# Where tiles stand in on-chip memory: 256-byte lines, and transposed activations 64 or 192 bytes behind a line

## The chip, the cores and the metric

The kernel runs on one core of one Trainium2 chip. The core has five engines with instruction queues of their own: TensorE (PE: matrix multiplies; its weight loads are shown apart as PEld), VectorE (DVE), ScalarE (ACT), GpSimd (POOL) and SyncE (SP), which here only issues DMAs. Operands lie in on-chip memory (SBUF, 128 partitions), matmul results in PSUM. The metric is the device time of one execution in microseconds (us).

## The reference

One layer of a bidirectional encoder on a sequence of 1024 tokens with 1024 features, in float32:

```python
a = rmsnorm(h, norm_mix[l])
proj = a @ w_in[l]
y_att = windowed_gqa(aq, ak, av, attn_sink[l]) @ w_branch_attn[l]
y_gla = gla_branch(gq, gk, gv, gr, z_f, z_b, ...) @ w_branch_gla[l]
merged = jax.nn.sigmoid(g_att) * y_att + jax.nn.sigmoid(g_gla) * y_gla
h = h + merged @ w_out[l]
h = h + expert_choice_ffn(rmsnorm(h, norm_ffn[l]), w_router[l], w_exp_gate[l], w_exp_up[l], w_exp_down[l])
ple_gate = jax.nn.sigmoid(rmsnorm(h, norm_ple[l]) @ w_ple_gate[l])
h = h + ple_gate * (p[l] @ w_ple[l])
return rmsnorm(h, norm_final)
```

`windowed_gqa` is attention with 8 query and 2 key heads in a window of 128 tokens, `gla_branch` a chunked linear attention with 4 heads in both directions, and `expert_choice_ffn` lets each of 16 experts take 128 tokens and run a SwiGLU of width 1024 on them. The experts' weights alone are 16 x 12 MB.

## The kernel before

**Split products.** Every large product is computed with three matmuls on the type float32r (`mm3`, lines 108 to 111): an operand x is kept as a pair, hi (x rounded by a ScalarE cast) and lo = x - hi (a VectorE subtraction), and hi·hi, hi·lo and lo·hi are summed in PSUM. `split` (lines 105 and 106) makes the pair, so line 106 stands for nearly all casts and subtractions of the profile. Tiles of such a pair end in `_h` and `_l` (`xt_h`, `xt_l`), weights are `wh`, `wl` or `slot`.

**A matmul and its two operands.** Each matmul instruction comes with a weight load: the stationary operand (128 columns, here 512 bytes of each partition) is loaded into the array, and the moving operand (512 or 256 columns) streams through it. In a profile's row the names behind the arrow are "moving,stationary" in most rows (`slot,xt_h`: the weight piece moves, xt_h is stationary); the two are put in another order in a few (`aT_h,wh`: aT_h moves). While one matmul streams, the weight load of the next one runs.

**Stages.** (1) Norm and transposition of the input into `aT_h`, `aT_l`; key, value and query projections with 256 moving columns of weights and aT stationary (`proj_tok`); gate projections with 512 columns of aT moving and weights stationary (`proj_T`). (2) Windowed attention, and the product of its transposed output `atT` with its branch weights (`m1_half`). (3) Four heads of linear attention, with more `proj_tok` and `proj_T`. (4) The second branch product and the product with w_out, both of whose operands are `slot` tiles; router; choice of tokens. (5) 16 experts: for each, 128 tokens are gathered into `xg`, transposed on TensorE and split into the pair `xt`; gate and up products (xt stationary, weight pieces moving, 512 columns) give `hid`, which is transposed and split into `hT`; the down product (hT stationary) is scaled and added into DRAM by an indirect DMA. Weight pieces of 1 MB come through a ring of 17 raw buffers (`next_pool`, line 1160), loaded by SP as a buffer comes free, and are split by ACT, DVE and some by POOL. (6) The last gate with pair `nT` as stationary operand, and the final norm.

**Order of the work.** Each engine runs its queue in the order in which the code is written; tiles come from pools, which are stacked in memory from the left and from the right side, and a tile that takes another's place waits for the last reader of that one.

**Where tiles stand.** The class `Lines` (lines 36 to 51) wraps a pool and rounds each tile up to a multiple of 128 bytes per partition, so that every tile begins on a multiple of 128 bytes; the tiles `edge` and `edge_small` shift the pools on both sides to such a line. The pool `small` is left as it is. In the program as built, 1209 tiles begin 128 bytes above a multiple of 256 and 645 on a multiple of 256. The 128x8x128 pairs and the weight pieces are all in the first class, with these exceptions: `atT`, the query weights in the pool `wqp`, and `v_h`, `sh`, `sl`, `qT` of the attentions.

Of the kernel before, what the change touches and what calls it, by code (L numbers as in the profile page):

```python
# [9 lines left out]
F32 = mybir.dt.float32  # L10
F32R = mybir.dt.float32r
BF16 = mybir.dt.bfloat16
I32 = mybir.dt.int32
# [7 lines left out]
T = 1024  # L21
NT = 8
D = 1024
KC = 8
EPS = 1e-6
NE = 16
INV_FREQ = [float(500000.0 ** (-i / 8.0)) for i in range(8)]
C_QA, C_KA, C_QG, C_KG, C_VG, C_RG, C_Z, C_GA, C_GG = 0, 512, 768, 1280, 1792, 2816, 3840, 3872, 4896

EDGE_SMALL = 24
SIZE = {F32: 4, F32R: 4, I32: 4, BF16: 2, U8: 1}


class Lines:
# [2 lines left out]
    def __init__(self, pool):  # L39
        self.pool = pool  # L40

    def tile(self, shape, dt, **kw):
        n = math.prod(shape[1:])
        per = 128 // SIZE[dt]
        if n % per == 0:
            return self.pool.tile(shape, dt, **kw)
        t = self.pool.tile([shape[0], -(-n // per) * per], dt, **kw)[:, 0:n]
        if len(shape) == 2:
            return t
        names = "abc"[:len(shape) - 1]  # L50
        return t.rearrange(f"p ({' '.join(names)}) -> p {' '.join(names)}", **dict(zip(names, shape[1:])))


@contextmanager
def lines(pool):
    with pool as p:
        yield Lines(p)
# [3 lines left out]
def tile_hybrid_block(  # L61
# [14 lines left out]
    def pool(name, bufs=1, side=None, space=None):  # L76
        kw = {}
        if side:
            kw["side"] = side
        if space is not None:  # L80
            kw["space"] = space
        if space != DRAM:
            kw["reuse_waits"] = "tile"
        made = tc.tile_pool(name=name, bufs=bufs, **kw)
        return made if space is not None or name == "small" else lines(made)


    ctx.enter_context(tc.tile_pool(name="edge", bufs=1, side="right")).tile([128, 24], F32, name="edge")
# [1 line left out]
    small = ctx.enter_context(pool("small", bufs=3))  # L90
# [7 lines left out]
    def bank(tag="mm"):  # L98
        return ps.tile([128, 512], F32, tag=tag, name="ps_" + tag, bufs=BUFS[tag])
# [48 lines left out]

    sA = ExitStack()
    aT_pool = sA.enter_context(pool("aT", side="right"))  # L150
    aT_h = aT_pool.tile([128, KC, T], F32R, name="aT_h")
    aT_l = aT_pool.tile([128, KC, T], F32R, name="aT_l")


    sinkb = const.tile([128, 8], F32, name="sinkb")
# [300 lines left out]
    with pool("lp") as lp:  # L456
        one = lp.tile([128, 128], F32, name="one")
        nc.gpsimd.memset(one, 1.0)
        for h in range(4):
# [14 lines left out]
            for u in (3, 2, 1, 0):  # L474
                nc.vector.tensor_sub(lt[:, u], lm[:, u], lt[:, u])
                for c in range(4):
                    ls = slice(c * 128, c * 128 + 128)
                    a, b = lm[:, u, ls], lt[:, u, ls]
                    if c >= 2:
                        a, b = a[:, ::-1], b[:, ::-1]  # L480
# [12 lines left out]
    ap2 = sB.enter_context(pool("at2", bufs=2))  # L493
# [13 lines left out]
    atT = {}  # L507

    def attn_block(b):
        lo_b, hi_b = max(0, b - 1), min(NT - 1, b + 1)  # L510
        nk = hi_b - lo_b + 1
        if b % 4 == 0:
            atT[b // 4] = (ap2.tile([128, 4, 512], F32R, name="atT_h", bufs=1),
                           ap2.tile([128, 4, 512], F32R, name="atT_l", bufs=1))
        ah, al = atT[b // 4]
        qhl = qT[b]
        ks = slice(lo_b * 128, (hi_b + 1) * 128)
        n = nk * 128
        sinks = [v.rearrange("p (g c) -> p g c", g=2) for v in (sinkb, nsink)]
        for cp in range(2):  # L520
# [31 lines left out]
            for g in range(2):  # L552
                for c in range(2):
                    nc.vector.tensor_scalar(sm[g][c][:, 0:n], sm[g][c][:, 0:n], rd[:, g, c:c + 1],
                                            None, op0=ALU.mult)
# [523 lines left out]
            merge(srt)  # L1079
    sO.close()  # L1080
    eg = ctx.enter_context(pool("eg", bufs=2))


    gtl = o1.tile([NE, 2, 128], F32, name="gtl")
# [18 lines left out]
    for t in range(NT - 1):  # L1103
        n = NT - 1 - t
# [12 lines left out]
    st = {}  # L1117

    def tokens(e):
        oh = eg.tile([128, NT, 128], BF16, name="oh", bufs=1)  # L1120
        nc.vector.tensor_tensor(oh, posT[:, :, e:e + 1].to_broadcast([128, NT, 128]),
                                iot.unsqueeze(1).to_broadcast([128, NT, 128]), op=ALU.is_equal)
        pi = bank("a")
        for t in range(NT):
            nc.tensor.matmul(pi[:, 0:2], oh[:, t], tok[:, t], start=t == 0, stop=t == NT - 1)
        idx = eg.tile([128, 1], I32, name="idx", bufs=NE)
        ins = nc.vector.tensor_scalar(idx, pi[:, 0:1], pi[:, 1:2], None, op0=ALU.add).ins
        st[e] = dict(idx=idx)
        return ins
# [7 lines left out]
    for e in range(2):  # L1137
        found = tokens(e)
        if e == 0:
            gathered = gather(0)  # L1140
    gather(1)
    tokens(2)


# [10 lines left out]
    e2 = sE.enter_context(pool("e2", side="right"))  # L1155
# [8 lines left out]
    def transposed(src, th, tl, g):  # L1164

        pt = bank("tr")
        for c in range(4):
            nc.tensor.transpose(pt[:, c * 128:(c + 1) * 128],  # L1168
                                src[:, (g * 4 + c) * 128:(g * 4 + c + 1) * 128], ident)
        split(th[:, g * 4:g * 4 + 4], tl[:, g * 4:g * 4 + 4], pt.rearrange("p (c t) -> p c t", c=4))  # L1170
# [18 lines left out]
    def hl_pair(po, name, **kw):  # L1189
        return [po.tile([128, KC, 128], F32R, name=name + x, **kw) for x in ("_h", "_l")]  # L1190

    def begin(e, after=None):
        st[e]["xt"] = hl_pair(e2, "xt")
        col = st[e]["col"] = eg.tile([128, NE + 1], F32, name="col", bufs=NE)
        with tc.issue_after(after) if after else ExitStack():
            nc.scalar.copy(col, st[e]["xg"][:, D:TW])
        for g in range(2):
            transposed(st[e]["xg"], *st[e]["xt"], g)

    begin(0)  # L1200
    for e in range(NE):
        s = st[e]
        hid = e2.tile([128, D], F32, tag="hid", name="hid", bufs=2)
        hT = hl_pair(e2, "hT")
        for c in range(2):
            cc = slice(c * 512, c * 512 + 512)
            pg = bank("mm")
            for k2 in range(2):
                part(pg, s["xt"], w_eg[e], k2, c)
            silu = nc.scalar.activation(hid[:, cc], pg, AF.Silu, scale=s["col"][:, NE:NE + 1])  # L1210
            pu = bank("mm")
            for k2 in range(2):
                part(pu, s["xt"], w_eu[e], k2, c)
            nc.vector.scalar_tensor_tensor(hid[:, cc], pu, s["col"][:, NE:NE + 1], hid[:, cc], op0=ALU.mult, op1=ALU.mult)
            transposed(hid, *hT, c)
        pd = [bank("b"), bank("b")]
        for c in range(2):
            part(pd[c], hT, w_ed[e], 0, c)
            if c == 0 and e + 1 < NE:
                begin(e + 1, silu.ins)  # L1220
        if e + 2 < NE:
            gather(e + 2)
        if e + 3 < NE:
            tokens(e + 3)
        y = e2.tile([128, D], F32, tag="hid", name="y", bufs=2)
        for c in range(2):
            part(pd[c], hT, w_ed[e], 1, c)
            nc.scalar.mul(y[:, c * 512:c * 512 + 512], pd[c], s["col"][:, e:e + 1])
        nc.gpsimd.indirect_dma_start(out=h_d[:, :], in_=y, in_offset=None, compute_op=ALU.add,
                                     out_offset=bass.IndirectOffsetOnAxis(ap=s["idx"][:, 0:1], axis=0))  # L1230
# [18 lines left out]
    f2 = ctx.enter_context(pool("f2", bufs=2, side="right"))  # L1249
# [23 lines left out]

    def front(t):
        ht = hs_[t]
        nT = hl_pair(f2, "nT")
        for g in range(2):
            transposed(ht, *nT, g)
        junk = f2.tile([128, D], BF16, name="junk", bufs=1)
        ss = small.tile([128, 1], F32, name="ssf")  # L1280
        nc.scalar.activation(junk, ht, AF.Square, accum_out=ss)
        rs = rstd_of(ss, D)
        rh = small.tile([128, 1], F32, name="rsh", bufs=4)
        nc.vector.tensor_scalar(rh, rs, 0.5, None, op0=ALU.mult)
        F[t] = ht, nT, rh
# [65 lines left out]
```

## Time and profile before

| | |
|---|---|
| median of 3 runs | 1777.96 us (1777.29 to 1778.06) |
| the profiled execution: its own time | 1777.2 us |
| its span from first to last instruction | 1775.5 us |
| mean granted TensorE clock | 0.984 of 2.4 GHz |
| PE busy | 1670.3 us, 94% of the span |
| DVE, ACT, POOL busy | 1223.0, 930.0, 259.6 us |

A matmul's busy time in the profile is longer than the distance to the next one, because matmuls overlap in the pipeline and their ends are modelled. What one matmul costs is therefore read from starts: the time from the start of one to the start of the next in an unbroken run, which is called the pitch here. The timeline shows starts to 0.01 us, so a run of n matmuls gives its mean pitch to 0.01/n us.

### The profile page before, as it was taken

The numbers are of one execution on the slowest core, as the hardware profiler recorded it, in microseconds if no ns is written. First come the engines' busy times: TensorE is split into PE (matmuls) and PEld (weight loads), VectorE is DVE, ScalarE is ACT, GpSimd is POOL, SyncE is SP. The second block draws the span as 40 slices with busy tenths as digits, with TensorE's granted clock in tenths as the row PEclk, the third lists the DMA queues.
The fourth block names the chain that finished last, engine by engine and source line by source line (L and its number), as shares of the span: only waits on it lengthen the run. The fifth ranks groups of instructions, "written<-read, shape, count | busy, mean of one in ns | idle before, by whom it ended". The sixth has DMA issues, their size and how long they took to land.

```text
span 1775.5 us, 23683 instructions
## 1 busy us (share of the span) xinstructions
PE 1670.3 (94%) x8795; PEld 1355.7 (76%) x8795; DVE 1223.0 (69%) x2412; ACT 930.0 (52%) x1451; POOL 259.6 (15%) x233
## 2 busy tenths in 40 slices
PE   7998999999999999999988849999999999999997
PEld 6977766768898989888866637777777777777786
DVE  7546855542646464663458888888989889888776
ACT  4245555341525252541222227787877878777742
POOL 1013300000000000000034232112221121221110
PEclk9999999999999999999999969999999999999999
DMA  6032411415212121065442569999999999994611
GB/s 226 1 102 107 131 32 40 144 49 187 70 50 72 49 71 49 1 208 172 157 177 108 204 230 380 375 373 366 373 357 370 377 368 369 347 372 151 224 62 48
DMA packets 171740, 335.10 MB, mean 189 GB/s; under 512 B 9180, under 2 KB 41988, under 8 KB 171624
## 3 DMA queue, kind: packets, MB, share of 16 engines
q1 hardware_dynamic: 154912, 277.96, 44.5%
q0 software_dynamic: 14704, 53.17, 9.2%
q10 hardware_dynamic: 2008, 2.46, 0.4%
q8 instruction: 69, 1.13, 0.3%
q14 instruction: 47, 0.39, 0.1%
HBM read 290.50 MB, written 43.06 MB: 188 GB/s over the span
## 4 chain that ended last, share of the span: by engine, by line
PE 75%; DVE 13%; issue 5%; ACT 4%; DMA 2%; POOL 1%; DVEq 0%; SPq 0%; ACTq 0%; POOLq 0%
PE ps_mm L111 17%; PE ps_mm L110 17%; PE ps_mm L109 16%; PE ps_b L110 5%; PE ps_b L111 5%; PE ps_b L109 5%; DVE slot L106 3%; ACT slot L106 2%; PE ps_tr L1168 2%; DVE lm L481 1%; DVE cand L918 1%; DVE rs_y L133 1%; PE ps_a L533 1%; PE ps_tr L562 1%; PE ps_b L567 1%
## 5 line engine op out<-in xcount | busy, mean ns | idle before, releaser
L106 DVE TENSOR_TENSOR slot<-slot 128x1024 fp32r<-128x1024 f32 x349 | 451.6, 1327 | 66.8 <-ACT slot L106 63.4
L106 ACT CAST slot<-slot 128x1024 fp32r<-128x1024 f32 x392 | 401.2, 1051 | 92.9 <-PE ps_mm L111 68.2
L110 PE MATMUL ps_mm<-slot,xt_h 128*128 128x512 f32 x512 | 203.7, 398 | 4.1 <-DVE slot L106 1.9
L111 PE MATMUL ps_mm<-aT_h,wl 128*128 128x512 f32 x512 | 203.2, 397 | 0.0
L109 PE MATMUL ps_mm<-aT_h,wh 128*128 128x512 f32 x512 | 202.1, 395 | 1.2 <-ACT sgr L246 1.2
L110 PE MATMUL ps_mm<-aT_l,wh 128*128 128x512 f32 x512 | 202.9, 396 | 0.0
L111 PE MATMUL ps_mm<-slot,xt_l 128*128 128x512 f32 x512 | 201.5, 394 | 0.0
L109 PE MATMUL ps_mm<-slot,xt_h 128*128 128x512 f32 x512 | 200.2, 391 | 0.0
L106 POOL TENSOR_TENSOR slot<-slot 128x1024 fp32r<-128x1024 f32 x43 | 104.2, 2425 | 417.5 <-ACT slot L106 230.1
L110 PEld LDWEIGHTS ps_mm<-slot,xt_h 128*128 128x128 f32 x512 | 96.5, 188 | 35.3 <-DVE slot L106 8.1
L109 PEld LDWEIGHTS ps_mm<-slot,xt_h 128*128 128x128 f32 x512 | 96.6, 189 | 20.2
L109 PEld LDWEIGHTS ps_mm<-aT_h,wh 128*128 128x128 f32 x512 | 96.7, 189 | 18.6 <-ACT sgr L246 1.4
L111 PEld LDWEIGHTS ps_mm<-slot,xt_l 128*128 128x128 f32 x512 | 96.5, 188 | 18.5
L111 PEld LDWEIGHTS ps_mm<-aT_h,wl 128*128 128x128 f32 x512 | 96.8, 189 | 18.1 <-issue 1.2
L110 PEld LDWEIGHTS ps_mm<-aT_l,wh 128*128 128x128 f32 x512 | 96.6, 189 | 18.2 <-issue 1.2
L106 DVE TENSOR_TENSOR wl<-raw,wh 128x2048 fp32r<-128x2048 f32 (+1 forms) x29 | 61.5, 2121 | 63.8 <-ACT wh L106 63.8
L110 PE MATMUL ps_b<-slot,hT_h 128*128 128x512 f32 x256 | 102.2, 399 | 0.8 <-POOL slot L106 0.7
L109 PE MATMUL ps_b<-slot,hT_h 128*128 128x512 f32 x256 | 102.5, 401 | 0.0
L111 PE MATMUL ps_b<-slot,hT_l 128*128 128x512 f32 x256 | 101.7, 397 | 0.0
L106 ACT CAST wh<-raw 128x2048 fp32r<-128x2048 f32 (+1 forms) x30 | 52.0, 1734 | 91.1 <-PE ps_mm L110 86.9
L109 PE MATMUL ps_mm<-wh,aT_h 128*128 128x256 f32 x320 | 92.4, 289 | 1.6 <-DVE sgr L588 1.6
L111 PE MATMUL ps_mm<-wh,aT_l 128*128 128x256 f32 x320 | 91.2, 285 | 1.4 <-DVE aT_l L106 1.4
(378 smaller groups left out, 3613.6 us busy)
## 6 DMA issues: line engine op xcount, KB each, us to landing
slot<-in_w_exp_down_dram SPq DMA_DIRECT2D x64, 1024.0 KB, 8.4
slot<-in_w_exp_gate_dram SPq DMA_DIRECT2D x62, 1024.0 KB, 8.0
slot<-in_w_exp_up_dram SPq DMA_DIRECT2D x62, 1024.0 KB
raw<-in_w_in_dram SPq DMA_DIRECT2D x16, 1024.0 KB, 7.3
raw<-in_w_in_dram SPq DMA_DIRECT2D x14, 512.0 KB, 5.3
sg_d<-sgr POOLq DMA_DIRECT2D x14, 512.0 KB, 3.0
xn_d<-xa POOLq DMA_DIRECT2D x8, 520.5 KB, 3.6
xt<-in_x_dram SPq DMA_DIRECT2D x8, 512.0 KB, 6.5
```

Source lines behind the costliest of these rows:

```text
L106: return nc.scalar.copy(hi, src), eng.tensor_sub(lo, src, hi)
L109: nc.tensor.matmul(out_ps, sh, mh, start=start, stop=False)
L110: nc.tensor.matmul(out_ps, sh, ml, start=False, stop=False)
L111: nc.tensor.matmul(out_ps, sl, mh, start=False, stop=stop)
L133: eng.scalar_tensor_tensor(y, t, c, y, op0=ALU.add, op1=ALU.mult)
L481: nc.vector.tensor_tensor_scan(a, one, b, 0.0, op0=ALU.mult, op1=ALU.add)
L533: nc.tensor.matmul(pss[g][:, 0:n], qhl[r, g, hc], kT_l[r, ks], start=False, stop=False)
L562: nc.tensor.transpose(pt[:, o:o + 128], sm[g][c][:, j * 128:(j + 1) * 128], ident)
L567: nc.tensor.matmul(po[r], va[:, lo_b + j, r], pT[:, g * 256:g * 256 + 256], start=j == 0, stop=j == nk - 1)
L918: nc.vector.match_replace(out=src[:, 0:n], in_to_replace=m8, in_values=src[:, 0:n], imm_value=-1.0)
L1168: nc.tensor.transpose(pt[:, c * 128:(c + 1) * 128], src[:, (g * 4 + c) * 128:(g * 4 + c + 1) * 128], ident)
```

## The change

Pools now round tiles up to multiples of 256 bytes, and `tile` takes an argument `behind`: the tile then begins so many bytes behind a line. Six pairs get one: aT and atT 192, xt 64, hT 192, nT 64. The tiles idx and col of the experts move from the pool `eg` into a pool `small_eg`, which is not rounded.

```diff
+LINE = 256
...
-    def tile(self, shape, dt, **kw):
+    def tile(self, shape, dt, behind=0, **kw):
         n = math.prod(shape[1:])
-        per = 128 // SIZE[dt]
-        if n % per == 0:
+        per, at = LINE // SIZE[dt], behind // SIZE[dt]
+        if n % per == 0 and not at:
             return self.pool.tile(shape, dt, **kw)
-        t = self.pool.tile([shape[0], -(-n // per) * per], dt, **kw)[:, 0:n]
+        t = self.pool.tile([shape[0], -(-(n + at) // per) * per], dt, **kw)[:, at:at + n]
...
-        return made if space is not None or name == "small" else lines(made)
+        return made if space is not None or name.startswith("small") else lines(made)
...
-    aT_h = aT_pool.tile([128, KC, T], F32R, name="aT_h")
-    aT_l = aT_pool.tile([128, KC, T], F32R, name="aT_l")
+    aT_h = aT_pool.tile([128, KC, T], F32R, name="aT_h", behind=192)
+    aT_l = aT_pool.tile([128, KC, T], F32R, name="aT_l", behind=192)
...
-            atT[b // 4] = (ap2.tile([128, 4, 512], F32R, name="atT_h", bufs=1),
-                           ap2.tile([128, 4, 512], F32R, name="atT_l", bufs=1))
+            atT[b // 4] = (ap2.tile([128, 4, 512], F32R, name="atT_h", bufs=1, behind=192),
+                           ap2.tile([128, 4, 512], F32R, name="atT_l", bufs=1, behind=192))
...
+    egs = ctx.enter_context(pool("small_eg", bufs=NE))
...
-        idx = eg.tile([128, 1], I32, name="idx", bufs=NE)
+        idx = egs.tile([128, 1], I32, name="idx")
...
-        st[e]["xt"] = hl_pair(e2, "xt")
-        col = st[e]["col"] = eg.tile([128, NE + 1], F32, name="col", bufs=NE)
+        st[e]["xt"] = hl_pair(e2, "xt", behind=64)
+        col = st[e]["col"] = egs.tile([128, NE + 1], F32, name="col")
...
-        hT = hl_pair(e2, "hT")
+        hT = hl_pair(e2, "hT", behind=192)
...
-        nT = hl_pair(f2, "nT")
+        nT = hl_pair(f2, "nT", behind=64)
```

What that does to the two operands of neighbouring matmuls, by the addresses in the two built programs (distance = address of the stationary operand that is being loaded minus address of the operand that is moving meanwhile, modulo 256 bytes):

| operand pair (moving, stationary) | columns moving | distance before | distance after |
|---|---|---|---|
| weight piece, xt | 512 | 0 | 64 |
| weight piece, hT | 512 | 0 | 192 |
| aT, weights (`proj_T`) | 512 | 0 | 64 |
| weights, aT (`proj_tok`) | 256 | 0; 128 for one of the two query pieces | 192 |
| weight piece, nT | 512 (last tile also 256) | 0 | 64 |
| atT, branch weights | 512 | 128 | 64 |
| slot, slot (branch and output products) | 512 | 0 | 0 |
| v_h, sh, sl with ktk, am, q pairs | 256 | 128 or 0 | 0 |

The order of the instructions on every engine is the same in both programs. Of the waits three differ. SP's first load into the buffer `rawD` (a piece of the first expert's down weights, third row) loses its wait on one DMA semaphore and on PE, because the pool now lies over other tiles. Before:

```order
119 L813 DMA slot<-in_w_exp_down_dram 128x4x512
120 L813 DMA slot<-in_w_exp_down_dram 128x4x512 [waits DMAHW2_49]
121 L813 DMA slot<-in_w_exp_down_dram 128x4x512 [waits DMASW1_49,DMASW3_49,PE_49,DMAHW4_49,Activation_49,Pool_49]
122 L813 DMA slot<-in_w_exp_gate_dram 128x4x512 [waits DMAHW5_49,PE_49]
123 L813 DMA slot<-in_w_exp_gate_dram 128x4x512 [waits DMAHW7_49,PE_49]
```

And SP at the same place after the change:

```order
119 L814 DMA slot<-in_w_exp_down_dram 128x4x512
120 L814 DMA slot<-in_w_exp_down_dram 128x4x512 [waits DMAHW2_49]
121 L814 DMA slot<-in_w_exp_down_dram 128x4x512 [waits DMASW1_49,DMAHW4_49,Activation_49,Pool_49]
122 L814 DMA slot<-in_w_exp_gate_dram 128x4x512 [waits DMAHW5_49,PE_49]
123 L814 DMA slot<-in_w_exp_gate_dram 128x4x512 [waits DMAHW7_49,PE_49]
```

Only the names in the brackets of row 121 differ; the other two differences are that this DMA wait is taken at SP's last load of h instead, and that one ACT wait on early loads is taken two tiles later in the router's stage.

## Rows read from the trace of the kernel before

**Rows 1.** The page: busy time, share of the span and instructions of each engine; then the shares of the chain that ended last, by engine and by line.

```profile
PE 1670.3 (94%) x8795; PEld 1355.7 (76%) x8795; DVE 1223.0 (69%) x2412; ACT 930.0 (52%) x1451; POOL 259.6 (15%) x233
...
PE 75%; DVE 13%; issue 5%; ACT 4%; DMA 2%; POOL 1%; DVEq 0%; SPq 0%; ACTq 0%; POOLq 0%
PE ps_mm L111 17%; PE ps_mm L110 17%; PE ps_mm L109 16%; PE ps_b L110 5%; PE ps_b L111 5%; PE ps_b L109 5%; DVE slot L106 3%; ACT slot L106 2%; PE ps_tr L1168 2%; DVE lm L481 1%; DVE cand L918 1%; DVE rs_y L133 1%; PE ps_a L533 1%; PE ps_tr L562 1%; PE ps_b L567 1%
```

**Rows 2.** Groups of PE instructions by line with shapes kept apart: line, engine, operation, out<-operands, array, shape, count | busy us, mean ns | idle before. Line 110 stands for each product's three lines 109 to 111, which have the same count.

```profile
L110 PE MATMUL ps_mm<-slot,xt_h 128*128 128x512 f32 x512 | 203.7, 398 | 4.1 <-DVE slot L106 1.9 <-POOL slot L106 1.8
...
L110 PE MATMUL ps_mm<-aT_l,wh 128*128 128x512 f32 x512 | 202.9, 396 | 0.0
...
L110 PE MATMUL ps_b<-slot,hT_h 128*128 128x512 f32 x256 | 102.2, 399 | 0.8 <-POOL slot L106 0.7
...
L110 PE MATMUL ps_mm<-wl,aT_h 128*128 128x256 f32 x320 | 91.4, 286 | 0.0
...
L110 PE MATMUL ps_mm<-slot 128*128 128x512 f32 x192 | 77.5, 404 | 0.0
...
L110 PE MATMUL ps_mm<-slot,nT_h 128*128 128x512 f32 x120 | 47.2, 393 | 0.0
...
L110 PE MATMUL ps_b<-slot 128*128 128x512 f32 x96 | 37.6, 392 | 1.0 <-DVE slot L806 1.0
...
L110 PE MATMUL ps_b<-wl,aT_h 128*128 128x256 f32 x128 | 36.5, 285 | 0.0
...
L110 PE MATMUL ps_mm<-atT_l,wh 128*128 128x512 f32 x64 | 25.7, 401 | 0.0
```

**Rows 3.** Timeline of PE in the expert stage (start us, length us): first and last of 28 matmuls of 512 columns in an unbroken run, distance 0.

```profile
1318.75 0.39 PE L109 MATMUL ps_b<-slot,hT_h 128*128 128x512 f32 x1
...
1324.87 0.39 PE L109 MATMUL ps_mm<-slot,xt_h 128*128 128x512 f32 x1
```

**Rows 4.** The same timeline just before, behind the transposes and the small token products: first and last of 11 matmuls, distance 0.

```profile
1316.22 0.39 PE L110 MATMUL ps_b<-slot,hT_h 128*128 128x512 f32 x1
...
1318.53 0.39 PE L111 MATMUL ps_b<-slot,hT_l 128*128 128x512 f32 x1
```

**Rows 5.** Timeline of PE in the attention's branch product: first and last of 10 matmuls of 512 columns, distance 128.

```profile
331.61 0.40 PE L111 MATMUL ps_mm<-atT_h,wl 128*128 128x512 f32 x1
...
333.70 0.39 PE L111 MATMUL ps_mm<-atT_h,wl 128*128 128x512 f32 x1
```

**Rows 6.** Timeline of PE, 256 columns, aT stationary. The first two: first and last of 20 matmuls with the second query piece, distance 128. The other two: first and last of 21 matmuls at distance 0.

```profile
36.02 0.28 PE L110 MATMUL ps_b<-wl,aT_h 128*128 128x256 f32 x1
...
38.27 0.28 PE L111 MATMUL ps_b<-wh,aT_l 128*128 128x256 f32 x1
...
78.07 0.28 PE L109 MATMUL ps_mm<-wh,aT_h 128*128 128x256 f32 x1
...
80.47 0.28 PE L111 MATMUL ps_mm<-wh,aT_l 128*128 128x256 f32 x1
```

**Rows 7.** Timeline of PE at the start of the first expert, while the granted clock was 0.5: first and last of 6 matmuls, distance 0.

```profile
1059.37 0.63 PE L110 MATMUL ps_mm<-slot,xt_h 128*128 128x512 f32 x1
...
1061.51 0.52 PE L109 MATMUL ps_mm<-slot,xt_h 128*128 128x512 f32 x1
```

**Rows 8.** The product with the narrow weights wzp (32 and 64 columns in turn): two weight-load groups of the view of one line (duration ns min/median/max), then the first of its 32 matmuls in the timeline and the matmul behind the last.

```profile
L420 PEld LDWEIGHTS ps_mm<-aT_l,wzp x14: 107/108/112, 117.2 to 123.6; 128*32 128x32 f32 x14
...
L421 PEld LDWEIGHTS ps_mm<-aT_h,wzp x16: 133/133/138, 116.7 to 123.8; 128*64 128x64 f32 x16
...
116.95 0.39 PE L421 MATMUL ps_mm<-aT_h,wzp 128*64 128x512 f32 x1
...
124.27 0.39 PE L109 MATMUL ps_mm<-aT_h,wh 128*128 128x512 f32 x1
```

**Rows 9.** Groups of PEld by line: the weight loads of xt_h with 128 columns (busy us, mean ns).

```profile
L110 PEld LDWEIGHTS ps_mm<-slot,xt_h 128*128 128x128 f32 x512 | 96.5, 188 | 35.3 <-DVE slot L106 8.1
```

**Rows 10.** One stretch of the expert stage, 14 experts: busy us and instructions of each engine, granted clock, DMA share, GB/s; and the GB/s of that stretch in 40 slices.

```profile
1080.00:1600.00 520.00, 500.55 (x2330) 396.64 (x2330) 460.33 (x414) 406.95 (x462) 108.84 (x56) 1.00 1.04 368
...
GB/s 386 384 372 386 331 398 388 335 390 388 315 388 389 348 387 376 337 393 371 351 387 338 375 386 342 400 384 316 390 388 325 387 390 344 377 338 358 392 354 357
```

**Rows 11.** Waits in the same stretch: engine, line waited for, us in total, times, longest. First PE's, then ACT's longest.

```profile
PE ps_tr L1168 <- DVE hT_l L106: 9.2, 12, 1.6
PE ps_tr L1168 <- DVE hid L1214: 8.8, 12, 0.8
PE ps_mm L110 <- POOL slot L106: 1.8, 3, 0.6
...
ACT slot L106 <- PE ps_mm L111: 32.0, 93, 0.6
```

**Rows 12.** Waits of the DMA queue of SP between 985 and 1100 us.

```profile
SPq L813 <- DMA h_d<-ht: 7.1, 1, 7.1
SPq L813 <- PE ps_b L111: 6.7, 1, 6.7
```

## Prediction

> **What bounds the kernel now.** I read the page first. PE is busy for 1670.3 of 1775.5 us, and its matmuls in lines 109 to 111 alone make up some 65% of the chain that ended last [rows 1]; PE has about 105 us without work in the whole span. In the 520 us of the expert stage PE is busy for 500.6, DVE for 460.3, ACT for 407.0 [rows 10], and PE's three largest waits there are 9.2, 8.8 and 1.8 us, while ACT waits 32.0 us for PE [rows 11]. So PE sets the end nearly everywhere, and the others follow. The change issues the same instructions in the same order; what it can alter is how long a matmul takes. Hence the second view, the groups by line, for the counts [rows 2], and the third, the timeline, for the pitch.
>
> A matmul of 512 columns in an unbroken run costs (1324.87 - 1318.75) / 27 = 0.2267 us [rows 3]. At half the clock the same product costs (1061.51 - 1059.37) / 5 = 0.428 us [rows 7], that is 512 columns at 1.2 GHz (0.4267) and nothing more; half of 0.427 is 0.2135. So at 2.4 GHz each matmul pays an excess of 13.2 ns. With 256 columns it is the same: (80.47 - 78.07) / 20 = 0.1200 against 0.1067, 13.3 ns [rows 6]. Behind a break (transposes, token products) the pitch is (1318.53 - 1316.22) / 10 = 0.231 [rows 4] and takes some ten matmuls to settle at 0.2267. I use 0.228 as the mean of both for 512 columns, an excess of 14.5 ns, and 13.3 ns for 256.
>
> Does the place of the operands matter? Yes: at distance 128 the 512-column matmul costs (333.70 - 331.61) / 9 = 0.2322 [rows 5], 5.5 ns more than at distance 0, and the 256-column one (38.27 - 36.02) / 19 = 0.1184 [rows 6], 1.6 ns less. No run before has a distance of 64 or 192.
>
> **The change part by part.** *The pairs at a new distance.* Counts are three times those of line 110 [rows 2]. 512 columns: xt 1536, aT moving 1536, hT 768, nT 360, atT 192, together 4392. 256 columns: aT stationary 3 x (320 + 128) = 1344 (nT's last tile adds a few dozen, left out). The slot-slot products, 3 x (192 + 96) = 864 matmuls, keep distance 0.
>
> What a matmul costs at 64 or 192 no row shows, so I bound it. Best case: the whole excess is two operand reads getting in each other's way, and it goes. That is 4392 x 14.5 ns = 63.7 us and 1344 x 13.3 ns = 17.9 us, 82 us. Worst case: the new distance acts as 128 does. Then 512 columns cost 5.5 ns more than settled, or 4.2 over my mean, and 256 cost 1.6 less: +18.4 (with atT's 192 left alone, 4200 x 4.2 = 17.6) - 2.1 = about +16 us; if 256 columns suffer like 512, +17.6 + 1344 x 4.2 = +23 us. Between ends so far apart the rows give no nearest neighbour: distances 0 and 128 are both 64 away. I take a third of the excess as gone: 4.8 ns for 512 columns (a pitch of 0.223) and 4.4 for 256 (0.1156). Three reasons for this side: an excess that doesn't grow with the columns (13.2 and 13.3 ns) and vanishes at half the clock looks like a clash at the start of each stream and not like a rate; the distance moves it by -1.6 to +5.5 ns, so it isn't fixed; and it doesn't settle at one value behind a break, so it depends on how the two reads fall against each other. One against: a load of 32 or 64 columns, which takes 107 to 133 ns and not 188 [rows 8, 9], leaves the pitch at (124.27 - 116.95) / 32 = 0.2288 [rows 8], so it isn't the length of the load that is paid; that is why I take a third and not all.
>
> Sum: 4392 x 4.8 = 21.1 us, 1344 x 4.4 = 5.9 us, 27.0 us of PE work. Where PE waits for another engine a faster matmul only waits longer: of the 27 I count 85%, since these matmuls stand on the chain for about 65% of the span (1154 us) where all products of lines 109 to 111 take some 1360 us (4392 + 864 at 0.228, 1344 at 0.12). That leaves 23 us.
>
> *What follows in the expert stage.* Per expert PE takes 144 x 4.8 ns = 0.7 us less of about 37. DMA must then move 368 x 37 / 36.3 = 375 GB/s on the mean, where slices reach 400 [rows 10]; the ring of 17 buffers covers dips. DVE's share goes from 460.3 / 520 = 89% to 90%. Neither becomes the bound; in the best case (2.1 us less per expert, 390 GB/s, DVE at 94%) both come close, and PE's waits for hT and hid [rows 11] would grow.
>
> *Tiles that go from distance 128 to 0* (v_h, sh, sl in the linear attention, 256 columns): by rows 6 1.6 ns each the wrong way; a few hundred matmuls, under 1 us. *Evictions into the shifted pairs* by ACT and DVE: nothing, or up to the same size either way as on PE, but DVE has 60 us to spare in the stretch of rows 10, so it is covered. *idx and col in small_eg*: the same operations, nothing. *The lost SP wait and the two moved ones*: SP waited 7.1 and 6.7 us in that neighbourhood [rows 12], but PE waited for no DMA of weights [rows 11], so an earlier load is only earlier in the ring: nothing. If PE did depend on that load, up to 7 us would go.
>
> Together: 1777.2 - 23 = 1754 us for the profiled execution, which is 0.8 us below the median of the runs shown; so 1755 for a median.
>
> The Trainium skill's page "SBUF — State Buffer", section "Who interferes with whom", says that TensorE has one read port for the moving operand and one for the weights, independent, and that PE and ACT never wait on anyone. By it the distance changes nothing; rows 5 and 6 against rows 3 speak against that, since the distance is what differs between them. The page "TensorE: Matmul & The Clock Gate", section "Back-to-back issue gap", gives N / 2.4 + 2.5 ns for one matmul behind another at full clock, 215.8 ns for 512 columns; the trace has 226.7 [rows 3]. If the new distance brought it there, the sum would be 85% of 4392 x 12.2 + 1344 x 10.8 ns, 58 us, an estimate from that page.
>
> **The rivals.** *Nothing happens.* The 13 ns are a fixed cost of changing weights, the same for every distance that isn't unlucky. For it: the short loads [rows 8]; the settled pitch, the same to 0.1 ns in 27 steps. Against it: rows 5 and 6. Then only atT changes, 192 x 5.5 ns = 1 us, and 1777 us result. The skill's rule on independent ports would have it so. *Most of the excess goes.* Two thirds or more of 82 us x 85% = 70: 45 to 70 us, 1708 to 1733 us. For it: the half clock, at which the excess is nil with the same two reads. Against it: rows 8. *It gets worse.* At 64 and 192 the two reads never settle as they do at 0, and each matmul costs what it costs behind a break (0.231) or at distance 128 (0.232), in place of 0.2267. The place is above all the expert stage and the gate projections, whose long runs are settled now; the price is +3 to +4.2 ns on 4200 matmuls and up to as much on 1344, 12 to 23 us on PE, which count nearly in full where PE has no waits: 1788 to 1800 us. It decides from a pitch of 0.229 in those runs. For it: of the two distances seen, the one other than 0 is worse for 512 columns. Against it: the 256-column run at 128 is better.
>
> **How the numbers follow.** The forecast, a part of the excess goes (7 to 45 us, 1733 to 1771): 0.40, because it is the middle of what rows 5 to 7 allow. Most goes: 0.16. Nothing, within 3.5 us (0.2%, about what a measurement of this kernel can tell from no change): 0.18. Worse: 0.26. So faster 0.56, same 0.18, slower 0.26. The range for 8 in 10 leaves out the better half of "most goes" and the tail of "worse": 1718 to 1798 us. The forecast's own range is 1735 to 1769.
>
> **What would show each step.** In the changed kernel's timeline an unbroken run of xt or hT matmuls at a pitch of 0.223 shows the forecast; 0.2267 shows the fixed cost; 0.229 or more the worse case; 0.216 the best. The slot-slot products must stay at 0.2267, which tells distance from other causes. proj_tok should show about 0.116. PE's busy time must fall by some 27 us and its waits for DVE hardly grow; if they grow by more than 5 us in the stretch of rows 10, the 85% was wrong. The prediction is wrong as a whole if xt, hT and aT with distances 64 and 192 behave differently from each other, since I gave all one price.

## The result, and the profile after

The changed kernel takes 1785.95 us (median of 6 runs, 1779.68 to 1791.75), the kernel before 1777.32 us beside it. The ratio is 1.0052, 95% interval [1.0029, 1.0075]: slower by half a per cent, where I had forecast faster by more than one. The profiled execution after has a span of 1784.0 us, its own time is 1785.76 us, its mean granted clock 0.981 (before 0.984).

The page of after, the lines that answer to [rows 1]:

```profile
PE 1683.7 (94%) x8795; PEld 1354.3 (76%) x8795; DVE 1220.7 (68%) x2412; ACT 929.1 (52%) x1451; POOL 258.4 (14%) x233
...
PE 74%; DVE 13%; issue 6%; ACT 4%; DMA 1%; POOL 1%; DVEq 0%; SPq 0%; ACTq 0%; POOLq 0%
```

The same 8795 instructions keep PE busy 13.4 us longer; every other engine is busy for as long as before, within 2.3 us. So the cost sits in the matmuls themselves. The groups by line with shapes apart show in which, beside [rows 2] (columns as there; line 111 of the changed kernel is line 110 of the one before):

```profile
L111 PE MATMUL ps_mm<-slot,xt_h 128*128 128x512 f32 x512 | 206.9, 404 | 3.6 <-POOL slot L107 1.8 <-DVE slot L107 1.7
...
L111 PE MATMUL ps_mm<-aT_l,wh 128*128 128x512 f32 x512 | 206.0, 402 | 0.0
...
L111 PE MATMUL ps_b<-slot,hT_h 128*128 128x512 f32 x256 | 102.7, 401 | 0.7 <-POOL slot L107 0.7
...
L111 PE MATMUL ps_mm<-wl,aT_h 128*128 128x256 f32 x320 | 89.5, 280 | 0.0
...
L111 PE MATMUL ps_mm<-slot 128*128 128x512 f32 x192 | 77.5, 403 | 0.0
...
L111 PE MATMUL ps_mm<-slot,nT_h 128*128 128x512 f32 x120 | 47.8, 398 | 0.0
```

xt, aT and nT with 512 columns are up by 5 to 6 ns a matmul, hT by 2, the slot pairs hardly move (404 and 403), and the 256-column products of `proj_tok` are down by 6. A mean duration here holds a modelled end; the pitch from start to start is the firmer number. In the timeline of PE these are the first and last matmul of five unbroken runs:

```profile
1320.78 0.39 PE L110 MATMUL ps_b<-slot,hT_h 128*128 128x512 f32 x1
...
1325.36 0.40 PE L112 MATMUL ps_b<-slot,hT_l 128*128 128x512 f32 x1
1325.59 0.39 PE L110 MATMUL ps_mm<-slot,xt_h 128*128 128x512 f32 x1
...
1332.82 0.40 PE L111 MATMUL ps_mm<-slot,xt_h 128*128 128x512 f32 x1
...
849.69 0.39 PE L112 MATMUL ps_mm<-slot 128*128 128x512 f32 x1
...
894.57 0.39 PE L112 MATMUL ps_mm<-slot 128*128 128x512 f32 x1
...
423.83 0.28 PE L110 MATMUL ps_mm<-wh,aT_h 128*128 128x256 f32 x1
...
441.74 0.28 PE L112 MATMUL ps_mm<-wh,aT_l 128*128 128x256 f32 x1
...
1059.21 0.63 PE L112 MATMUL ps_mm<-slot,xt_l 128*128 128x512 f32 x1
...
1061.77 0.63 PE L112 MATMUL ps_mm<-slot,xt_l 128*128 128x512 f32 x1
```

- hT, distance 192: (1325.36 - 1320.78) / 20 = 0.2290 us.
- xt, distance 64: (1332.82 - 1325.59) / 31 = 0.2332, where [rows 3] has 0.2267 at distance 0.
- slot pairs, distance 0 before and after: (894.57 - 849.69) / 198 = 0.2267.
- `proj_tok` in the first head of the linear attention, distance 192: (441.74 - 423.83) / 158 = 0.1134, where [rows 6] has 0.1200. This run is not typical: by the starts of all unbroken pairs only 15% of `proj_tok` took 115 ns or less in this execution, and the mean is 117.1 (table below).
- xt at half the clock: (1061.77 - 1059.21) / 6 = 0.4267, as in [rows 7]. At the lower clock the distance costs nothing.

Over the whole trace, the mean pitch of neighbouring matmuls of equal width that wait for nothing, at full clock, worked out from the starts of all 8795 records:

| pair, columns | distance before, after | ns before | ns after | matmuls x difference |
|---|---|---|---|---|
| xt, 512 | 0, 64 | 227.9 | 233.3 | 1536 x 5.4 = +8.3 us |
| aT moving, 512 | 0, 64 | 228.1 | 233.3 | 1536 x 5.2 = +8.0 |
| nT, 512 | 0, 64 | 227.3 | 233.4 | 360 x 6.1 = +2.2 |
| hT, 512 | 0, 192 | 229.2 | 230.2 | 768 x 1.0 = +0.8 |
| atT, 512 | 128, 64 | 232.8 | 233.3 | 192 x 0.5 = +0.1 |
| `proj_tok`, 256 | 0 (one piece 128), 192 | 119.8 | 117.1 | 1344 x -2.7 = -3.6 |
| slot pairs, 512 | 0, 0 | 227.8 | 227.8 | 0 |

The sum is +15.8 us on PE; about 9 us of it reach the end. In the expert stage, the rows that answer to [rows 10] and [rows 11]:

```profile
1080.00:1600.00 520.00, 501.08 (x2307) 393.15 (x2306) 454.35 (x409) 403.39 (x458) 108.15 (x56) 1.00 1.04 363
```

```profile
ACT slot L107 <- PE ps_mm L112: 38.8, 117, 0.5
...
PE ps_tr L1170 <- DVE hT_l L107: 9.5, 12, 1.4
PE ps_tr L1170 <- DVE hid L1216: 8.2, 12, 0.7
...
PE ps_mm L111 <- POOL slot L107: 1.2, 2, 0.6
```

PE is as full as before (501.08 us against 500.55) and gets through 23 matmuls fewer; ACT waits 38.8 us for it instead of 32.0. So the other engines, too, wait for PE and don't set the time there.

### The profile page after: what moved, and what is told of

Same layout as the page of the kernel before. It is cut to its first block, busy times and chain, and to the rows that moved or that the text cites. A ratio compares the mean times of both kernels' runs of the same rounds, so it can differ in the third digit from the quotient of the medians.

```text
span 1784.0 us, 23683 instructions
## 1 busy us (share of the span) xinstructions
PE 1683.7 (94%) x8795; PEld 1354.3 (76%) x8795; DVE 1220.7 (68%) x2412; ACT 929.1 (52%) x1451; POOL 258.4 (14%) x233
## 4 chain that ended last, share of the span: by engine, by line
PE 74%; DVE 13%; issue 6%; ACT 4%; DMA 1%; POOL 1%; DVEq 0%; SPq 0%; ACTq 0%; POOLq 0%
PE ps_mm L112 17%; PE ps_mm L111 16%; PE ps_mm L110 16%; PE ps_b L111 5%; PE ps_b L112 5%; PE ps_b L110 5%; DVE slot L107 4%; ACT slot L107 3%; PE ps_tr L1170 2%; DVE cand L919 1%; PE ps_a L534 1%; DVE rs_y L134 1%; PE ps_tr L563 1%; PE ps_b L568 1%; DVE lm L482 1%
## 5 line engine op out<-in xcount | busy, mean ns | idle before, releaser
L111 PE MATMUL ps_mm<-slot,xt_h 128*128 128x512 f32 x512 | 206.9, 404 | 3.6 <-POOL slot L107 1.8
L110 PE MATMUL ps_mm<-slot,xt_h 128*128 128x512 f32 x512 | 203.5, 398 | 0.0
```

What stands on the lines that cost most here:

```text
L110: nc.tensor.matmul(out_ps, sh, mh, start=start, stop=False)
L111: nc.tensor.matmul(out_ps, sh, ml, start=False, stop=False)
```

## The experiments

Theory 1: the distance sets the pitch, and its sign depends on the number of moving columns. Theory 2: the distance is a bystander, and something else in the change costs the time (coarser lines, the new pool, a lost or moved wait).

**sweep.** A bench: 60 matmuls in a row for each distance between the two operands, with no engine but PE at work meanwhile.

```diff
+    for d in range(0, 256, 16):
+        run("wide_" + at[d // 16], 512, 0, d)
+    for d in range(0, 256, 16):
+        run("half_" + at[d // 16], 256, 0, d)
```

> This kernel computes none of the reference: it runs matmuls alone, 60 in a row for each distance between stationary and moving operand (0 to 240 bytes in steps of 16, letters a to p), with 512 and with 256 moving columns, and a few other cases, with no other engine at work; its output is filled with zeros. Theory 1, the distance sets the pitch by itself and its sign depends on the columns: 512 columns give 0.2267 us at distance 0, about 0.233 at 64, 0.228 to 0.230 at 192, 0.2325 at 128; 256 columns give 0.120 at 0, 0.1135 at 64, 0.117 at 192, 0.1185 at 128. Theory 2, in the large kernel other engines' traffic or the placing of single tiles made the difference: then every distance gives 0.2267 and 0.120 here. A load of 32 columns: if only the length of overlap counted, the pitch at 64 would be nearly that at 0; if it is a matter of the start of the two reads, it stays apart. Both operands moved by 64 at distance 0 must give 0.2267 if distance alone counts. bf16, with half the bytes per column: near 0.216 at every distance if the excess belongs to 4-byte columns at full clock.

The timeline of PE merges each case into one row; the last letter is the distance in steps of 16 bytes (a 0, b 16, e 64, f 80, m 192, n 208), and the pitch is the difference to the next start, over 60:

```profile
31.45 13.76 PE L75 MATMUL ps_wide_a<-mov,sta 128*128 128x512 f32 x60
45.05 13.77 PE L75 MATMUL ps_wide_b<-mov,sta 128*128 128x512 f32 x60
...
86.64 14.15 PE L75 MATMUL ps_wide_e<-mov,sta 128*128 128x512 f32 x60
100.64 14.08 PE L75 MATMUL ps_wide_f<-mov,sta 128*128 128x512 f32 x60
...
198.40 13.90 PE L75 MATMUL ps_wide_m<-mov,sta 128*128 128x512 f32 x60
212.14 14.16 PE L75 MATMUL ps_wide_n<-mov,sta 128*128 128x512 f32 x60
...
253.75 7.35 PE L75 MATMUL ps_half_a<-mov,sta 128*128 128x256 f32 x60
260.94 7.26 PE L75 MATMUL ps_half_b<-mov,sta 128*128 128x256 f32 x60
...
282.21 6.98 PE L75 MATMUL ps_half_e<-mov,sta 128*128 128x256 f32 x60
289.02 7.29 PE L75 MATMUL ps_half_f<-mov,sta 128*128 128x256 f32 x60
...
381.10 13.78 PE L75 MATMUL ps_wide_moved<-mov,sta 128*128 128x512 f32 x60
394.72 14.06 PE L75 MATMUL ps_wide_thin_a<-mov,sta 128*32 128x512 f32 x60
408.62 14.06 PE L75 MATMUL ps_wide_thin_e<-mov,sta 128*32 128x512 f32 x60
422.52 10.58 PE L75 MATMUL ps_most_a<-mov,sta 128*128 128x384 f32 x60
...
491.25 13.12 PE L75 MATMUL ps_bf_a<-movb,stab 128*128 128x512 bf16 x58
504.21 13.11 PE L75 MATMUL ps_bf_e<-movb,stab 128*128 128x512 bf16 x59
517.16 13.11 PE L75 MATMUL ps_bf_i<-movb,stab 128*128 128x512 bf16 x59
```

512 columns: (45.05 - 31.45) / 60 = 0.2267 us at 0, 0.2333 at 64, 0.2290 at 192. 256 columns: 0.1198 at 0, 0.1135 at 64. Of 16 distances with 512 columns none is under 0.2266, so distance 0, where the kernel before stood, is the floor; with 256 columns 0 is among the slowest (119.8 to 120.0, as at 112, 160 and 240). 384 columns lie between: 173.4 ns at 0 and 192, 176.7 at 64. At 128 columns the pitch settles at 111.6 at all four distances tried. Both operands moved by 64 bytes together settle at 226.7 again (0.2270 over all 60): the distance counts, not the address. The bench's other steps are multiples of 512 bytes; that 256 counts as 0 shows in the kernel before, where by the addresses of the built program xt stands 256 bytes from its weight pieces modulo 512 and nearly all slot pairs stand at 0, and both settle at 0.2267. With a stationary operand of 32 columns the pitch is 0.2317 at 0 and at 64. In bf16 the pitch is (504.21 - 491.25) / 60 = 0.216 at 0 and the same at 64, 128 and 192. The Trainium skill's page "TensorE: Matmul & The Clock Gate", section "Back-to-back issue gap", gives N / 2.4 + 2.5 ns as the gap of a single, isolated matmul, 215.8 ns for 512 columns; the bf16 runs agree with it, the runs in this kernel's 4-byte type don't. The Trainium skill's page "SBUF — State Buffer", section "Who interferes with whom", gives TensorE independent read ports for the two operands; the bf16 runs agree with that, and the 4-byte runs speak against it, since their pitch depends on how the two operands stand to each other. Where in the chip they meet no run shows.

**lines.** All `behind` arguments taken out (five pairs have one: aT, atT, xt, hT and nT); the lines of 256 bytes, the new pool and the changed waits stay. By the built programs every instruction has the same waits as in the changed kernel.

```diff
-    aT_h = aT_pool.tile([128, KC, T], F32R, name="aT_h", behind=192)
+    aT_h = aT_pool.tile([128, KC, T], F32R, name="aT_h")
...
-        st[e]["xt"] = hl_pair(e2, "xt", behind=64)
+        st[e]["xt"] = hl_pair(e2, "xt")
```

> The changed kernel with every pair put back on its line (256-byte lines and small_eg stay). Theory 1 (distance): the 9 us go, since xt, hT, nT and aT are at distance 0 again; only atT (128 to 0, 192 x 5.5 ns = 1 us better) and one query piece (128 to 0, under 1 us worse) differ from before: 1776 to 1778 us, pitch of unbroken xt runs 0.2267. Theory 2 (the pools, their waits or the coarser lines cost the time): it stays at 1784 to 1787 us.

1775.98 us, ratio to before 1.0000 [0.9991, 1.0009]. Theory 2 falls: coarser lines, pool and waits together cost nothing that can be measured (within 0.1%).

**only_a and only_experts.** The first shifts aT and atT alone, the second xt, hT and nT alone.

```diff
     # only_a
+    aT_h = aT_pool.tile([128, KC, T], F32R, name="aT_h", behind=192)
...
     # only_experts
+        st[e]["xt"] = hl_pair(e2, "xt", behind=64)
...
+        hT = hl_pair(e2, "hT", behind=192)
```

> The changed kernel in which only aT and atT stay 192 bytes behind a line; xt, hT and nT are back on it. Theory 1: proj_tok gains 1344 x 2.8 ns = 3.8 us, proj_T loses 1536 x 5.2 ns = 8.0 us on PE, of which part stands beside other work; by the starts of the same matmuls in the two traces the sum up to 830 us was about 0: 1776 to 1780 us. Theory 2: as the changed kernel, 1784 to 1787.

> The changed kernel in which only xt (64), hT (192) and nT (64) stay behind a line; aT and atT are back on it. Theory 1: xt loses 1536 x 5.4 ns = 8.3 us, hT 768 x 1.0 = 0.8, nT 360 x 6.1 = 2.2, about 11 us on PE, of which the traces showed some 7 to 9 us at the end: 1784 to 1788 us. A rival, that the loss came from the projections and a change of granted clock there: 1777.

only_a: 1778.31 us, 1.0008 [0.9999, 1.0017]. only_experts: 1783.03 us, 1.0044 [1.0030, 1.0058]. only_a alone can't be told from no change. The two add up to the whole (0.08% + 0.44% against 0.52%). By the table above aT pays little because it loses 8.0 us on 1536 matmuls of 512 columns and wins 3.6 on 1344 of 256.

**tok64.** What theory 1 suggests: everything of 512 columns stays at distance 0, and the weights that `proj_tok` moves stand 192 bytes behind a line, which makes its distance 64.

```diff
-        w_v = piece([(0, w_in[:, C_VG + h * 256:C_VG + (h + 1) * 256])])
+        w_v = piece([(0, w_in[:, C_VG + h * 256:C_VG + (h + 1) * 256])], behind=192)
```

(and so for the key and value piece and both query pieces)

> All activations on a line again, and instead the weights that proj_tok reads as moving operand (the key and value piece, both query pieces, the value piece of each GLA head) 192 bytes behind one, so that the 1344 matmuls of 256 columns have distance 64 and everything of 512 columns keeps distance 0. Theory 1 (the pitch follows from distance and number of columns): 1344 x (119.9 - 113.4 = 6.5 ns) = 8.7 us less on PE, of which 60 to 90% come through because part of these matmuls stands beside work of the other engines: 1769 to 1772 us beside 1776 to 1777 of before, ratio 0.995 to 0.997. Theory 2 (the lines and pools, not the distance, made the difference): no change, ratio 1.000.

1770.40 us, ratio to before 0.9969 [0.9957, 0.9981]: faster than both kernels. But the pitch of `proj_tok` was 116.8 ns on the mean, not the bench's 113.4. So the time met its range while the term behind it was less than half its size in the profiled execution: 3.9 us less on PE, not 8.7. That it came out right is in part luck.

**tok64_gla.** The same, and v_h, v_l, sh and sl of the linear attention behind a line too.

```diff
-        v_h = g2.tile([128, NT, 256], F32R, name="v_h")
+        v_h = g2.tile([128, NT, 256], F32R, name="v_h", behind=192)
```

> As the run before it, and v_h, v_l, sh and sl of the GLA heads, the moving operands of 420 further matmuls of 256 columns, 192 bytes behind a line as well (distance 64). Theory 1 with PE as the bound there: 420 x 6.5 ns = 2.7 us at most, some 1 to 2 us less than the run before it, 1767 to 1771 us. If the GLA part is bounded by the waits between PE, DVE and ACT and not by PE's pitch: the same time as the run before it.

1770.27 us, 0.9967 [0.9956, 0.9978]: no different from tok64. In the profiles the unbroken pairs of these matmuls, some 330, went from 119.5 to 118.3 ns only, 0.4 us in all; so this run doesn't show whether waits between PE, DVE and ACT would have swallowed a larger gain.

**fine.** A second bench, with steps of 4 bytes, and with pairs in which the distance to a matmul's own stationary operand differs from that to the next one.

```diff
+    run("wide_own", 512, (0, 64), (0, 64))
+    run("wide_next", 512, (64, 0), (0, 64))
```

> This kernel computes nothing of the reference: a bench of runs of 60 matmuls, its output is zeros. It asks two things. First, which operand pair sets the pitch: in the run called own the moving operand and its own stationary both alternate between 0 and 64 bytes, so the distance to the own stationary stays 0 and the distance to the stationary that is loaded meanwhile (the next one) is 64 or 192; in the run called next it is the other way round. If the operand read beside the load counts (theory 1 as I have stated it), own gives about 231 ns at 512 columns (the mean of 233.3 and 228.8) and about 115.6 at 256 (the mean of 113.4 and 117.8), and next gives 226.7 and 120. If a matmul's own pair counts, the two change places. Second, how sharp the levels are: distances from 0 to 28 and from 184 to 248 in steps of 4 bytes at 512 columns, from 48 to 80 at 256, and 320 and 448 columns at 0 and 64. Theory 1 expects plateaus (226.7 up to 16 bytes, 233.3 from 32) rather than a point at exactly 0, and the gain of distance 64 at 256 columns to turn into a loss somewhere between 320 and 448 columns.

```profile
345.31 14.05 PE L76 MATMUL ps_wide_own<-mov,sta 128*128 128x512 f32 x60
359.20 14.16 PE L76 MATMUL ps_wide_next<-mov,sta 128*128 128x512 f32 x60
373.20 7.17 PE L76 MATMUL ps_half_own<-mov,sta 128*128 128x256 f32 x60
380.20 7.16 PE L76 MATMUL ps_half_next<-mov,sta 128*128 128x256 f32 x60
387.20 8.96 PE L76 MATMUL ps_three<-mov,sta 128*128 128x320 f32 x60
```

By the starts, over 60: own gave 231.5 ns at 512 columns and 116.7 at 256, next 233.3 and 116.7. In next the distance as it was defined ahead (to the operand that is loaded meanwhile) is 0, and the pitch still isn't 226.7. So neither pair alone sets the pitch, and distance 0 is good for 512 columns only where it holds for both; in the kernel the two distances are equal modulo 256. I don't know which reads meet. There are no plateaus either: 232.4 at 4 bytes, 230.8 at 8, 233.4 at 16. 320 columns cost 146.7 at 0 and 64, 448 columns 202.7 and 202.1, so the gain and the loss don't simply turn over between 320 and 448. The surprise was that figures of the first bench didn't return: distance 16 gave 233.4 (226.7 in sweep), 256 columns at 64 gave 117.8 (113.4 in sweep). What came just before differed in the two benches. That gave theory 3: at most distances more than one pitch can hold, and a run keeps the one it falls into.

**modes.** Runs of 24 matmuls at one distance that begin in five ways.

```diff
+    def case(name, n, d, lead, w):
...
+        steps = [lead] * 8 if lead is not None else []
+        steps += [d] * 24
...
+        nc.scalar.copy(junk[:, 0:w], t[:, 0:w])
```

> This kernel computes nothing of the reference: a bench of runs of 24 matmuls, each behind a break in which PE waits for ACT to read the sums of the run before, its output is zeros. The runs of one distance and width begin in five ways: behind a break of one of three lengths (x, y, z), or behind 8 matmuls of the same width at distance 0 (near) or 64 (far). Theory 1 (the distance alone sets the pitch): all five give the same pitch, at 512 columns 226.7 at distance 0, 233.3 at 64, 128 and 16 or 226.7 at 16, at 256 columns 120 at 0 and one figure for 64. Theory 3 (at most distances more than one pitch can hold, and a run keeps the one it falls into): the same distance gives different pitches for different beginnings; at 512 columns distance 16 gives 226.7 near and 233 far, at 256 columns distance 64 gives 113.4 for some beginnings and 118 for others, while 512 columns at distance 0 fall into 226.7 and 512 columns at 64 into 233 whatever came before.

Timeline rows (start, length): 256 columns at distance 64 (e) and 192 (g), behind a break (x, 24 matmuls), behind 8 at distance 0 (near) and 8 at 64 (far, both 32 matmuls):

```profile
317.60 2.99 PE L89 MATMUL ps_half_e_x<-mov,sta 128*128 128x256 f32 x24 [0.41 <-ACT junk L90]
...
327.96 4.05 PE L89 MATMUL ps_half_e_near<-mov,sta 128*128 128x256 f32 x32 [0.52 <-ACT junk L90]
332.42 3.91 PE L89 MATMUL ps_half_e_far<-mov,sta 128*128 128x256 f32 x32 [0.41 <-ACT junk L90]
...
356.39 3.09 PE L89 MATMUL ps_half_g_x<-mov,sta 128*128 128x256 f32 x24 [0.41 <-ACT junk L90]
...
367.06 3.94 PE L89 MATMUL ps_half_g_near<-mov,sta 128*128 128x256 f32 x32 [0.52 <-ACT junk L90]
```

By the starts of the last 16 matmuls of each run, distance 64 holds 113.3 ns behind a break and 117.8 behind matmuls at distance 0; distance 192 the other way round, 117.8 and 113.3. In the rows: e_x takes 0.10 us less than g_x for the same 24 matmuls, e_far 0.14 less than e_near. 512 columns have no such choice where it matters here: 226.6 to 227.4 at 0 and 233.3 to 233.4 at 64 from all five beginnings. Theory 3 holds for 256 columns. For 512 it is open at distance 16, which gave 233.3 both near and far: the eight matmuls at distance 0 in near had not settled (225 to 240 ns apart behind the first pair), while in sweep distance 16 followed 60 that had, so that beginning was not tried again. At 52 bytes 256 columns came to 113.3 from four beginnings; behind the fifth, matmuls at distance 0, the last 16 took 114.1 on the mean.

**tok52 and tok64_again.** The hope that a distance with one good pitch in the bench keeps it in the kernel.

```diff
-    w_v = piece([(0, w_in[:, C_VG + h * 256:C_VG + (h + 1) * 256])], behind=192)
+    w_v = piece([(0, w_in[:, C_VG + h * 256:C_VG + (h + 1) * 256])], behind=204)
```

> As the run tok64, with the proj_tok weights 204 bytes behind a line and not 192, so that the 1344 matmuls of 256 columns have distance 52. In the bench of beginnings distance 52 fell into 113.3 ns from all five, distance 64 only from four. Theory 3 (which pitch holds depends on the distance and on how the run begins): proj_tok at about 113.5 ns in nearly all runs where it was 116.8 in tok64, 1344 x 3.3 = 4.4 us less on PE, of which 60 to 90% come through: 1766 to 1768 us, 0.995 to 0.996 of before. If the bench's beginnings are not those of the kernel, or a start off the 64-byte steps costs the engines that write these weights something: 1770 us or more, proj_tok at 116 to 118 ns.

> The kernel of the run tok64 once more, beside tok52 on the same chip. Both theories: 0.996 to 0.998 of before, about 1770 us, proj_tok at 116 to 118 ns on the mean; which of its runs fall into 113.3 and which into 118 may differ from the first time.

tok52: 1773.70 us, 0.9984 [0.9975, 0.9993]; tok64_again: 1770.14 us, 0.9959 [0.9945, 0.9972]. The hope failed: `proj_tok` ran at 118.6 ns in tok52. In tok64_again its mean was 115.0, under the 116 to 118 that I had expected. Why the kernel doesn't fall where the bench did stays open. These are the timelines of the same head's value product, first and last matmul of an unbroken run, in tok64, in tok64_again (the same kernel) and in tok52:

```profile
423.75 0.28 PE L110 MATMUL ps_mm<-wh,aT_h 128*128 128x256 f32 x1
...
439.89 0.28 PE L112 MATMUL ps_mm<-wh,aT_l 128*128 128x256 f32 x1
```

```profile
423.83 0.28 PE L110 MATMUL ps_mm<-wh,aT_h 128*128 128x256 f32 x1
...
441.40 0.28 PE L112 MATMUL ps_mm<-wh,aT_l 128*128 128x256 f32 x1
```

```profile
423.75 0.28 PE L110 MATMUL ps_mm<-wh,aT_h 128*128 128x256 f32 x1
...
441.89 0.28 PE L110 MATMUL ps_mm<-wh,aT_h 128*128 128x256 f32 x1
```

The three stretches hold 138, 156 and 154 matmuls: 16.14 / 137 = 0.1178, 17.57 / 155 = 0.1134 and 18.14 / 153 = 0.1186 us. One and the same kernel ran this product at either pitch: in the first profile 23% of the unbroken `proj_tok` pairs took 115 ns or less, in the second 62%.

The best version I have is tok64: everything of 512 moving columns at distance 0, `proj_tok` at 64, 0.3 to 0.4% faster than before in both comparisons (intervals above), with a median some 15 us under that of the changed kernel.

## Why the prediction was wrong

**The step that failed** is "I take a third of the excess as gone: 4.8 ns for 512 columns (a pitch of 0.223) and 4.4 for 256". Measured: 5.2 to 6.1 ns more for 512 columns at distance 64, 1.0 more at 192, and 2.7 less for 256 columns at 192. In my own terms the -21.1 us of the 512 columns was +19.4, the -5.9 us of the 256 columns -3.6. The second half had the right sign at three fifths of its size; the first had the wrong sign.

**Why I chose that side.** I had read that 0 and 128 are both 64 bytes away and that the rows so give no neighbour. But they gave a sign for each width: at 128 the 512 columns were 5.5 ns worse and the 256 columns 1.6 better [rows 5, 6]. My "worst case: the new distance acts as 128 does" gave +16 us; the table's sum is +15.8. That the two sums are so close is luck, since their parts differ (xt +5.4 ns and hT +1.0 where I had put +4.2 for both, `proj_tok` -2.7 where I had put -1.6), but the signs were those of the rows. I had it as a bound and walked away from it towards a third of a best case that no row supported. My three reasons didn't carry: the excess at distance 0 is 13.3 ns at 256, 384 and 512 columns alike (sweep: 120.0, 173.4 and 226.7 less the columns at 2.4 GHz), it does vanish at half the clock, and it does move with the distance. But for 512 columns this 13.3 is the least that any distance tried gives. That the pitch takes some ten matmuls behind a break to settle [rows 3, 4] I read as room for a better place; it says nothing either way, since in modes 256 columns at distance 0 settle at 120.0, close to the worst, and 512 at 64 settle at 233.3. The reason against, that short loads leave the pitch as it is [rows 8], could not be read from those rows: by the addresses of the built program that product stands at distance 128, where full loads took 0.2322 [rows 5]. In sweep a load of 32 columns costs 0.2317 at distance 0, so there a shorter load is no gain.

**One price for all distances and both widths.** I wrote that the prediction is wrong as a whole if the distances behave differently from each other. They did: xt, hT and `proj_tok` went +5.4, +1.0 and -2.7 ns.

**The 85%.** The prediction let 85% of PE's change reach the end. Against lines, which has the same pools, the unbroken matmuls of after took 14.4 us more, those of only_experts 10.3, of only_a 4.5, of tok64 3.9 less (the sum of start-to-start differences, matmul by matmul, in the profiled executions). The times moved by +9.2, +7.8, +1.4 and -5.5 us (ratio times 1776). So of the whole change's cost 64% came through; the ratio's interval allows 36 to 92%, so the times alone don't rule out 85%. The traces show the loss: at the breaks, where PE waits anyway, after was 6.4 us shorter than lines, so a slower matmul partly eats its wait. For xt this is 2.2 of 8.0 us, and only_experts shows it again with 2.4 of 8.0. The two profiles differ by 9.6 us; the remaining 1.6 us come from the stretches of half clock, of which after had 68.4 us and lines 67.0. tok64's 5.5 us are more than its 3.9: one profile doesn't stand for all runs of a kernel whose `proj_tok` pitch differs between executions (116.8 and 115.0 ns in the two kept).

**What held.** The slot pairs stayed at 0.2267. PE's waits for DVE and POOL in the expert stage did not grow, DVE and DMA did not become the bound. idx, col, the lost SP wait and the coarser lines cost nothing (lines, 1.0000). The tiles that went from 128 to 0 cost nothing that can be measured: lines has them too.

**The rivals.** "It gets worse" was the right one, with its place and its point (a pitch of 0.229 or more in the long runs). Its price of 12 to 23 us on PE holds the table's 15.8; its time of 1788 to 1800 us was too high, since it let PE's cost count nearly in full. Its mechanism, "never settle as they do at 0", is half right: at 64 the 512 columns do settle, at 233.3. "Nothing happens" is refuted by sweep, and "most of the excess goes" by it too, for 512 columns.

## What to carry to other kernels

Where 4-byte matmuls of 128-row operands run back to back on PE, place the tiles so that the moving operand stands at the same address modulo 256 bytes as its own stationary operand and as the one being loaded meanwhile when 512 columns move, and apart (64 or 192 here) when 256 move; don't move one tile that is used both ways. Where the trace has a distance that is not yours, take its sign for each width as the forecast and the hoped-for gain as the rival, not the other way round. A bench prices all distances at once, but what it says of one that can hold two pitches has to be seen again in the kernel.

## What I had not expected of the hardware

- The pitch of 4-byte matmuls depends on the operands' distance modulo 256 bytes, in opposite ways for 512 columns (226.7 ns at 0, up to 235.0 elsewhere) and 256 (120.0 at 0, down to 113.3); in bf16 it is 216 at each of four distances. Both its own stationary operand and the one being loaded count (own and next in fine).
- At some distances two pitches can hold, and in the bench what ran just before picks one: 256 columns at 64 bytes keep 113.3 or 117.8 (modes), and one kernel shows both in the same product in two executions (tok64, tok64_again). What picks it there is not settled.
- With a stationary operand of 32 columns the pitch at 512 moving columns is 231.7 ns at distance 0 and at 64 (sweep), slower than with 128 columns at distance 0.
